# A hybrid attention block: last products of a stick-breaking pair moved behind the next pair's first units, and three kinds of DMA moved to another queue

## The chip, the cores and the metric

The kernel runs on one core of one Trainium2 chip. The metric is the time on the device in microseconds (us), the median of several runs. Before the change it is 1302.98 us (three runs, 1301.31 to 1303.53).

The core has five engines that run side by side and wait for each other by semaphores: PE (TensorE, matrix products and transposes, results in the banks of PSUM), DVE (VectorE), ACT (ScalarE), POOL (GpSimd) and SP (SyncE, which only issues DMAs here). Each engine goes through its own list of instructions in the order in which the program has them there. An instruction that waits holds what stands behind it in that list, and that goes for an instruction that issues a DMA too.

## The reference

One layer of a decoder: 1024 tokens, width 1024, all in float32.

```
h = rmsnorm(x);  proj = h @ w_in                      # 1024 x 3072
# group A, 8 heads of 64: q and k normed and rotated; three dilated branches
#   (window, dilation) = (128,1), (512,4), (2048,16), merged by their softmax denominators
# group B, 8 heads of 64, stick-breaking:
#   beta = sigmoid(q.k/8);  a[t,s] = beta[t,s] * prod_{s<j<t} (1 - beta[t,j]),  s < t;  o = a @ v
x = x + concat(rmsnorm(o_A), rmsnorm(o_B)) @ w_out
x = x + (silu(n @ w_gate) * (n @ w_up)) @ w_down      # n = rmsnorm(x), inner width 2816
```

## The kernel before

A float32 product is made of three products of rounded parts (`mm3`, lines 90 to 95: high by high, high by low, low by high), so each operand is first split by ACT (a copy that rounds) and DVE or POOL (the rest). The program runs in stages: norm and the projections of v, q and k of group A (to about 175 us of the profile), four pairs of heads of group A (175 to 362), four pairs of group B (348 to 588), the last output products and the second norm (to 659), the feed-forward part with Strassen-like combinations (649 to 1300).

The two attention groups use less of PE than the rest, so other products are mixed in as background: the projections of group B (`project_ahead`, tile pp) and the output products of group A (`merge_a`, tile yo). The main loop (lines 771 to 788) draws them from a generator: each `yield` of `attend_a` or `attend_b` reports how much of a pair is done, on a scale where a whole pair is about 24, and the loop lets background out in proportion (`RATES`), and the steps that prepare the next pair's q, k and v (`prep`, `FILL`). `hold` keeps a background product behind the score product that was written last before it.

The order of the instructions on an engine is not the order of the text. A planner (line 1186, `schedule_with_timeline_sim=True`) lays the whole program out along a modelled timeline when it is built; the text gives the priority, and what the model shows as ready goes first. So an instruction can stand ahead of one that the text has before it, and a transfer that takes longer than in the model holds what was placed behind it.

Group B, one pair of heads (`attend_b`, line 645). For each of 8 blocks of 128 queries and each head s a unit (`unit_b`, line 546) makes scores of n = 128 to 1024 keys (L430, L431, L433, tile sc), two sigmoids on ACT (L552, tiles kp and pb), a running product backwards over the keys on DVE (L555, the scan; its first operand is kp, the second is a column of zeros that is spread out, `aside`), and the product of the two, on POOL for s = 0 and on DVE for s = 1 (L556). kp has three buffers. Blocks go by twos, which are called groups g = 0 to 3; a group's four pb tiles are three of tag P (six buffers) and one of tag E (two). `ptpv` (line 559) then transposes the pb of a group (L572, tile pt), takes the transposes out of PSUM with ACT (L574, tile th) and multiplies them with v (L581, tile pv). In the text a group's `ptpv` comes after the next group's units, and the last group's at the end of the pair.

`aside` is one column in a PSUM bank of tag t. That tag has one bank, which group A uses as an accumulator; the bank is taken over at the start of the first pair of group B and filled by L649. In the last pair of group A the accumulator is taken out by L512.

Group A (`attend_a`, line 619). Per pair two halves of 512 queries, each in four steps. L449 and L450 make scores, DVE masks them and finds the maximum (L451), ACT takes the exponentials (L453), `turn_a` transposes (L498), takes out (L535, L537) and multiplies with v (L507). At the end of a half the sums and maxima are exchanged between layouts through DRAM (`factors`, line 455): st goes out (L460), comes back as x (L462), a few small operations make factors (`weigh`, L468 to L480), these go out (L481) and come back spread over partitions (`wide`, L486, two transfers). `finish` (line 611) multiplies on POOL (L615, L616) and stores the half (L617, tile oa). `weigh` and `finish` are due a fixed number of steps later (`WEIGH`, `USE`). All transfers of the kernel are issued by SP; the one at L462 waits for the two at L460, L486 for the one at L481, L617 for POOL. Behind them on SP stand, among others, the loads of rl, the stored projections for the next pair (L308, L311), which ACT and DVE turn into q and k (L339, L365, L340, L366), and the weights of the background (L69).

Of the kernel before, what the change touches and what calls it, by code (L numbers as in the profile page):

```python
# [11 lines left out]
F32 = mybir.dt.float32  # L12
FR = mybir.dt.float32r
AF = mybir.ActivationFunctionType
ALU = mybir.AluOpType
# [22 lines left out]
def tile_hybrid_block(ctx, tc, x, attn_norm_w, w_in, q_norm_w, k_norm_w, dil_w, sb_w,  # L38
                      w_out, ffn_norm_w, w_gate, w_up, w_down, cos, sin, amask, smask, out):
    nc = tc.nc  # L40

    big = ctx.enter_context(tc.tile_pool(name="big", bufs=1))

    def H(name, dtype=FR):
        return big.tile([128, 4, 512], dtype, tag="H", name=name, bufs=8)
# [4 lines left out]
    nc.vector.memset(ones, 1.0)  # L50
    mhalf = big.tile([128, 16], F32, name="mhalf")
    nc.vector.memset(mhalf, -0.5)
    def rstd_of(ss, n, pool, w):

        r = pool.tile([128, 16], F32, tag="rs", name="rs", bufs=6)
        nc.gpsimd.tensor_scalar(r[:, :w], ss, 1.0 / n, EPS, op0=ALU.mult, op1=ALU.add)
        nc.gpsimd.tensor_tensor(r[:, :w], r[:, :w], mhalf[:, :w], op=ALU.pow)
        return r
# [21 lines left out]
    def after(i, first, why, cls=mybir.DependencyClass.NoSync):  # L80

        tc.add_manual_dep(i.ins, first.ins.name,
                          mybir.DependencyInfo(cls, mybir.DependencyReason.DATA), reason=why)
# [47 lines left out]
    def P4(name, tag="P"):  # L131
        return att.tile([128, 1024], F32, tag=tag, name=name, bufs={"P": 6, "G": 2, "E": 2, "M": 1}[tag])
# [44 lines left out]
    def tok(w, tb, tag):  # L177

        p = PS.tile([128, 512], F32, tag, "va")
        c = slice((tb % 4) * 128, (tb % 4) * 128 + 128)  # L180
        for d in range(ND):
            h = hT[d // 4][tb // 4]
            mm3(p, (h[0][:, d % 4, c], h[1][:, d % 4, c]), (w[d // 2][0][:, d % 2, :], w[d // 2][1][:, d % 2, :]), d == 0, d == ND - 1)
        return p


    p = PS.tile([128, 512], F32, "s", "warm")
# [3 lines left out]
    for tb in range(NT):  # L191
# [14 lines left out]
        p = tok(wv, tb, "d")  # L206
        t = att.tile([128, 512], F32, tag="rq", name="rq", bufs=2)
# [20 lines left out]
    for nm, w in (("q", q_norm_w), ("k", k_norm_w)):  # L228
        t = P4("rope" + nm, "E").rearrange("p (s t e) -> p s t e", s=2, t=NT)
# [225 lines left out]
    def factors(st):  # L455


        sums = dram.tile([512, 2, 4], F32, name="sums")
        for l, order in enumerate(("(k p) l v -> p k l v", "(p k) l v -> p k l v")):
            nc.sync.dma_start(sums.rearrange(order, k=4)[:, :, l], st[:, l].rearrange("p k m s -> p k (m s)"))  # L460
        x = att.tile([128, 4, 2, 2, 2], F32, tag="x", name="x", bufs=2)
        nc.sync.dma_start(x.rearrange("p t l m s -> p t (l m s)"), sums.rearrange("(p t) l v -> p t (l v)", t=4))  # L462
        fac = dram.tile([2, 2, 512], F32, name="fac")

        def weigh():
            v = x.rearrange("p t l m s -> p l m s t")
            low = att.tile([128, 2, 4], F32, tag="low", name="low", bufs=2)
            i = nc.vector.tensor_tensor(low, v[:, 0, 0], v[:, 1, 0], op=ALU.min)  # L468
            after(i, gate[0], "the values are on their way")
            e = att.tile([128, 2, 2, 4], F32, tag="fe", name="fe", bufs=2)  # L470
            d = att.tile([128, 2, 2, 4], F32, tag="fd", name="fd", bufs=2)
            for l in range(2):
                nc.vector.tensor_tensor(e[:, l], low, v[:, l, 0], op=ALU.subtract)
            nc.scalar.activation(e, e, AF.Exp)
            for l in range(2):
                nc.vector.tensor_tensor(d[:, l], e[:, l], v[:, l, 1], op=ALU.mult)
            nc.vector.tensor_tensor(low, d[:, 0], d[:, 1], op=ALU.add)
            nc.vector.reciprocal(low, low)
            for l in range(2):
                nc.vector.tensor_tensor(e[:, l], e[:, l], low, op=ALU.mult)  # L480
            nc.sync.dma_start(fac.rearrange("l s (p t) -> p (l s) t", t=4), e.rearrange("p l s t -> p (l s) t"))  # L481

        def wide():
            t = P4("fac", "E").rearrange("p (l t) -> p l t", l=2)
            for s in range(2):
                nc.sync.dma_start(t[64 * s:64 * s + 64], fac[:, s].partition_broadcast(64))  # L486
            return t
        return weigh, wide

# [56 lines left out]
    def unit_b(pr, s, qb, tag):  # L546
        n = (qb + 1) * 128
        turn[0] += 1
        p, kp = P4("pb", tag), P4("kp", "GGM"[turn[0] % 3])
        for sp, c0, c1 in scores(pr, s, qb):  # L550
            for t, scale in ((kp, -0.125), (p, 0.125)):
                i = nc.scalar.activation(t[:, c0:c1], sp, AF.Sigmoid, scale=scale)  # L552
                after(i, last_exp[0], "one activation table at a time")
        rv = kp[:, n - 1::-1] if n == 1024 else kp[:, :n][:, ::-1]
        nc.vector.tensor_tensor_scan(rv, rv, aside[0][:, 0:1].to_broadcast([128, n]), 1.0, op0=ALU.mult, op1=ALU.bypass)  # L555
        (nc.gpsimd, nc.vector)[s].tensor_tensor(p[:, :n - 1], p[:, :n - 1], kp[:, 1:n], op=ALU.mult)  # L556
        return p

# [52 lines left out]
    def finish(pr, hf, o, wide):  # L611
        f = wide()
        t = pr.o[hf]
        for l in range(2):
            nc.gpsimd.tensor_tensor(t[l], t[l], f[:, l], op=ALU.mult)  # L615
        nc.gpsimd.tensor_tensor(t[0], t[0], t[1], op=ALU.add)  # L616
        nc.sync.dma_start(o[:, 512 * hf:512 * hf + 512], t[0])  # L617

    def attend_a(pr, o):

# [21 lines left out]

    aside = [None]

    def attend_b(pr, o):

        if aside[0] is None:
            aside[0] = PS.tile([128, 512], F32, "t", "aside")
            nc.vector.memset(aside[0][:, 0:1], 0.0)  # L649
        late = None  # L650
        for g in range(4):
            pq = []
            for k in range(2):
                pq.append([unit_b(pr, s, 2 * g + k, "PPPE"[2 * k + s]) for s in range(2)])
                catch_up(2)
                yield 0.2 * (2 * g + k + 1)
            if late:
                while pend:
                    catch_up(9)
                ptpv(*late)  # L660
                yield 0.92 * (2 * late[1] + 1.5)
            late = (pr, g, pq, o)
        ptpv(*late)
        yield 0.92 * (2 * late[1] + 1.5)

    def out_parts(g, i, hf, o, parts, acc):

# [139 lines left out]
    def wide(name, tag):  # L807
        t = att.tile([128, 1024], FR, tag=tag, name=name, bufs=BUFS[tag])
        return [t[:, 0:512], t[:, 512:1024]]
# [6 lines left out]
    for key, tags in (("b11", "PPPP"), ("b21", "PPvv")):  # L816
        t = [att.tile([128, 2, 512], FR, tag=tag, name=key, bufs=BUFS[tag]) for tag in tags]
# [78 lines left out]
    g = [None] * NF  # L896
# [143 lines left out]
    for ft in range(NF - LATE, NF):  # L1040
        gate_up(ft)
        if NF - 1 - ft < 12 - LATE:
            k = ft - (NF - 12 + LATE)
# [9 lines left out]
    sums = [H("tk", F32) for _ in range(4)]  # L1053
# [3 lines left out]
    for tag, n in (("k2", 2), ("k2", 2), ("kh", 4)):  # L1057
        t = att.tile([128, 1024], F32, tag=tag, name="lk", bufs=n)
# [131 lines left out]
```

## Time and profile before

| | |
|---|---|
| median of three runs | 1302.98 us |
| the profiled execution's own time | 1305.24 us |
| its span, first to last instruction | 1303.5 us |
| mean granted clock of PE | 0.991 |
| PE busy | 1265.4 us, 97% of the span |
| DVE, ACT, POOL busy | 840.0, 621.6, 384.2 us |
| DMA packets | 171.42 MB on SP's queue |

The profile tells one execution. A line of a group reads: program line, engine, operation, tiles (written <- read), shapes, count, busy time, mean of one in ns, then the idle time of the engine just before, and what ended most of it. In the order of time: start, length, engine, line, operation, tiles, and in brackets the idle time before it with what ended it. SPq is SP's queue of DMA issues. PEclk or "clock" is the share of PE's full rate that the chip granted. Since PE's instructions overlap, a busy PE can still be one at half rate.

### The profile page before, as it was taken

How to read it: one execution, taken by the hardware profiler on the slowest of the kernel's cores; microseconds unless marked ns; L12 is line 12 of the kernel's file. 1: busy time of each engine (PE TensorE's matmuls, PEld its weight loads, DVE VectorE, ACT ScalarE, POOL GpSimd, SP SyncE). 2: the span in 40 equal slices, each digit the busy share in tenths (PEclk: the TensorE clock that was granted, in tenths of full speed). 3: DMA queues.
4: the chain of work that ended last, by engine and by line, in shares of the span. 5: the costliest groups of instructions: out<-in, count | busy, mean ns of one | idle time of the engine just before them, and what ended most of it. 6: DMA issues, size and time to landing. Idle time of an engine off the chain costs nothing.

```text
span 1303.5 us, 18281 instructions
## 1 busy us (share of the span) xinstructions
PE 1265.4 (97%) x6260; PEld 1000.3 (77%) x6260; DVE 840.0 (64%) x1412; ACT 621.6 (48%) x1305; POOL 384.2 (29%) x330
## 2 busy tenths in 40 slices
PE   8999999999889988999999999999999999999998
PEld 6888887776666766767888888888888887788886
DVE  5333346566477768654798676665546878986775
ACT  5431267776687777753565222233333223444443
POOL 3488622422224234243312222321222321100000
PEclk9999999999989999999999999999999999999999
DMA  9633143544414253132246545323456448403532
GB/s 275 221 114 113 59 120 100 132 132 131 124 57 114 72 178 123 41 126 85 73 130 218 175 151 168 102 84 103 133 150 197 127 147 313 165 17 112 195 138 81
DMA packets 189326, 172.59 MB, mean 132 GB/s; under 512 B 33713, under 2 KB 134193, under 8 KB 189233
## 3 DMA queue, kind: packets, MB, share of 16 engines
q1 hardware_dynamic: 189232, 171.42, 41.8%
q8 instruction: 49, 0.80, 0.3%
q14 instruction: 45, 0.36, 0.1%
HBM read 133.96 MB, written 37.42 MB: 131 GB/s over the span
## 4 chain that ended last, share of the span: by engine, by line
PE 86%; ACT 4%; DVE 4%; DMA 3%; issue 2%; POOL 0%; SPq 0%; DVEq 0%; ACTq 0%; POOLq 0%
PE yd L1090 15%; PE gu L94 11%; PE gu L95 11%; PE gu L91 11%; PE va L95 3%; PE va L94 3%; PE va L91 3%; PE pp L91 3%; PE pp L94 3%; PE pp L95 3%; PE yo L91 2%; PE yo L94 2%; PE yo L95 2%; PE pv L507 2%; PE pv L581 2%
## 5 line engine op out<-in xcount | busy, mean ns | idle before, releaser
L864 ACT ACTIVATE wh<-wr 128x512 fp32r<-128x512 f32 x132 | 83.4, 632 | 210.0 <-PE gu L94 175.5
L94 PE MATMUL gu<-t,wh 128*128 128x512 f32 x352 | 139.0, 395 | 0.0
L91 PE MATMUL gu<-t,wh 128*128 128x512 f32 x352 | 138.8, 394 | 0.0
L95 PE MATMUL gu<-t,wl 128*128 128x512 f32 x352 | 138.8, 394 | 0.0
L1090 PE MATMUL yd<-dl,dh 128*128 128x512 f32 x308 | 121.7, 395 | 2.2 <-DVE dl L865 2.2
L1090 PE MATMUL yd<-dh,dl 128*128 128x512 f32 x308 | 121.2, 393 | 0.0
L94 PE MATMUL gu<-b,wh 128*128 128x512 f32 x264 | 104.5, 396 | 0.0
L91 PE MATMUL gu<-b,wh 128*128 128x512 f32 x264 | 104.3, 396 | 0.0
L95 PE MATMUL gu<-b,wl 128*128 128x512 f32 x264 | 104.2, 396 | 0.0
L555 DVE TENSOR_TENSOR_SCAN kp<-kp,aside 128x128 f32<-128x128 f32 (+7 forms) x64 | 85.4, 1347 | 27.3 <-ACT kp L552 26.9
L865 DVE TENSOR_TENSOR wl<-wr,wh 128x512 fp32r<-128x512 f32 x105 | 80.2, 763 | 8.1 <-ACT wh L864 8.1
L1090 PE MATMUL yd<-dh 128*128 128x512 f32 x308 | 84.6, 395 | 0.0
L91 PE MATMUL pp<-hh,wh 128*128 128x512 f32 x192 | 78.6, 410 | 0.0
L91 PEld LDWEIGHTS gu<-t,wh 128*128 128x128 f32 x352 | 66.2, 188 | 15.8
L94 PEld LDWEIGHTS gu<-t,wh 128*128 128x128 f32 x352 | 66.1, 188 | 15.7
L95 PEld LDWEIGHTS gu<-t,wl 128*128 128x128 f32 x352 | 66.1, 188 | 15.7
L91 PE MATMUL va<-wt,hh 128*128 128x512 f32 x192 | 76.5, 400 | 1.3 <-ACT wt L152 1.1
L864 ACT ACTIVATE dh<-wd 128x512 fp32r<-128x512 f32 x55 | 34.8, 632 | 90.2 <-PE yd L1090 83.6
L95 PE MATMUL va<-wt,hl 128*128 128x512 f32 x192 | 76.2, 398 | 0.7 <-DVE hl L62 0.7
L94 PE MATMUL va<-wt,hh 128*128 128x512 f32 x192 | 76.1, 399 | 0.2 <-DVE wt L153 0.2
L94 PE MATMUL pp<-hl,wh 128*128 128x512 f32 x192 | 76.3, 397 | 0.0
L95 PE MATMUL pp<-hh,wl 128*128 128x512 f32 x192 | 76.3, 397 | 0.0
(214 smaller groups left out, 3067.4 us busy)
## 6 DMA issues: line engine op xcount, KB each, us to landing
wd<-in_w_down_dram SPq DMA_DIRECT2D x88, 256.0 KB, 2.7
wr<-in_w_gate_dram SPq DMA_DIRECT2D x80, 256.0 KB, 3.0
wr<-in_w_up_dram SPq DMA_DIRECT2D x60, 256.0 KB, 3.0
raw<-in_w_in_dram SPq DMA_DIRECT2D x48, 256.0 KB, 4.3
raw<-in_w_out_dram SPq DMA_DIRECT2D x32, 256.0 KB, 2.9
raw<-rq SPq DMA_DIRECT2D x24, 256.0 KB, 2.6
g<-gu SPq DMA_DIRECT2D x20, 256.0 KB, 5.5
xt<-in_x_dram SPq DMA_DIRECT2D x8, 512.0 KB, 6.9
```

Source lines behind the costliest of these rows:

```text
L91: i = nc.tensor.matmul(ps, a[0], b[0], start=first, stop=False)
L94: nc.tensor.matmul(ps, a[0], b[1], start=False, stop=False)
L95: return nc.tensor.matmul(ps, a[1], b[0], start=False, stop=last)
L507: nc.tensor.matmul(pr.acc[lay][64 * s:64 * s + 64, cols], v[:, 64 * s:64 * s + 64], th[:, c:c + n], start=first, stop=last)
L555: nc.vector.tensor_tensor_scan(rv, rv, aside[0][:, 0:1].to_broadcast([128, n]), 1.0, op0=ALU.mult, op1=ALU.bypass)
L581: i = nc.tensor.matmul(pr.pv[64 * s:64 * s + 64, c - n:c], pr.v[:, j, 64 * s:64 * s + 64], th[:, n * s:n * s + n], start=j == 0, stop=j == ...
L864: nc.scalar.activation(h, r, AF.Copy)
L865: two(n).tensor_tensor(l, r, f(h), op=ALU.subtract)
L1090: mm = nc.tensor.matmul(pp[k], a[x][:, c], b[y], start=not more and j == 0 and x + y == 0, stop=j == HF - 1 and x == 1, skip_group_check=True)
```

## The change

Three things. The last group's `ptpv` of a stick-breaking pair is kept in `late` across pairs and written, for the first three pairs, after the next pair's group 0 of units; the last pair writes its own at the end. `part` scales what the pairs report as done, so that each still comes to 24: the first pair has one `ptpv` less, the last one more. `aside` is taken over at the start of group 2 of the first pair, and until then the scans read a column of zeros in SBUF, `zero`, instead. And three kinds of DMAs of group A, x (L462), fac (L486) and oa (L617), are issued by POOL instead of SP; L460 and L481 stay on SP.

```diff
+    zero = big.tile([128, 1], F32, name="zero")
+    nc.vector.memset(zero, 0.0)
...
-        nc.sync.dma_start(x.rearrange("p t l m s -> p t (l m s)"), sums.rearrange("(p t) l v -> p t (l v)", t=4))
+        nc.gpsimd.dma_start(x.rearrange("p t l m s -> p t (l m s)"), sums.rearrange("(p t) l v -> p t (l v)", t=4))
...
-                nc.sync.dma_start(t[64 * s:64 * s + 64], fac[:, s].partition_broadcast(64))
+                nc.gpsimd.dma_start(t[64 * s:64 * s + 64], fac[:, s].partition_broadcast(64))
...
-        nc.vector.tensor_tensor_scan(rv, rv, aside[0][:, 0:1].to_broadcast([128, n]), 1.0, op0=ALU.mult, op1=ALU.bypass)
+        nc.vector.tensor_tensor_scan(rv, rv, (aside[0] if aside[0] is not None else zero)[:, 0:1].to_broadcast([128, n]), 1.0, op0=ALU.mult, op1=ALU.bypass)
...
-        nc.sync.dma_start(o[:, 512 * hf:512 * hf + 512], t[0])
+        nc.gpsimd.dma_start(o[:, 512 * hf:512 * hf + 512], t[0])
...
+    late = [None]
+
     def attend_b(pr, o):
 
-        if aside[0] is None:
-            aside[0] = PS.tile([128, 512], F32, "t", "aside")
-            nc.vector.memset(aside[0][:, 0:1], 0.0)
-        late = None
+
+        part = 24.0 / (23.8 - 6.9 * (pr.i == 0) + 6.9 * (pr.i == 3))
         for g in range(4):
+            if aside[0] is None and g == 2 and pr.i == 0:
+                aside[0] = PS.tile([128, 512], F32, "t", "aside")
+                nc.vector.memset(aside[0][:, 0:1], 0.0)
             pq = []
             for k in range(2):
                 pq.append([unit_b(pr, s, 2 * g + k, "PPPE"[2 * k + s]) for s in range(2)])
                 catch_up(2)
-                yield 0.2 * (2 * g + k + 1)
-            if late:
+                yield part * 0.2 * (2 * g + k + 1)
+            if late[0]:
                 while pend:
                     catch_up(9)
-                ptpv(*late)
-                yield 0.92 * (2 * late[1] + 1.5)
-            late = (pr, g, pq, o)
-        ptpv(*late)
-        yield 0.92 * (2 * late[1] + 1.5)
+                ptpv(*late[0])
+                yield part * 0.92 * (2 * late[0][1] + 1.5)
+            late[0] = (pr, g, pq, o)
+        if pr.i == 3:
+            ptpv(*late[0])
+            yield part * 0.92 * (2 * late[0][1] + 1.5)
```

## The prediction

> **What bounds the kernel now.** I read the page first, for the engine that ends last, then the busy time by stage, then who ended PE's waits, and then the order of time around the longest of them. On the page the busy line and the shares of the chain are
>
> ```profile
> PE 1265.4 (97%) x6260; PEld 1000.3 (77%) x6260; DVE 840.0 (64%) x1412; ACT 621.6 (48%) x1305; POOL 384.2 (29%) x330
> PE 86%; ACT 4%; DVE 4%; DMA 3%; issue 2%; POOL 0%; SPq 0%; DVEq 0%; ACTq 0%; POOLq 0%
> ```
>
> PE is idle for 38.1 us of 1303.5. The change removes no product, so it can only win some of that, and whatever PE loses to a lower clock. The view by stretches shows where (length, busy us of each engine, PEclk near the end of the row). The dilated group is at work from 175 to 350, the stick-breaking pairs from 350 to 590; rows of it are
>
> ```profile
> core 0: us, PE busy (x) PEld busy (x) DVE busy (x) ACT busy (x) POOL busy (x), PEclk, DMA share, GB/s
> 175.00:300.00 125.00, 124.98 (x847) 96.42 (x845) 73.34 (x286) 95.80 (x281) 35.41 (x30) 1.00 0.45 117
> 300.00:350.00 50.00, 47.41 (x311) 35.49 (x310) 28.04 (x101) 33.42 (x100) 14.89 (x11) 0.97 0.40 118
> 350.00:367.00 17.00, 8.81 (x56) 6.24 (x55) 8.54 (x17) 9.96 (x22) 2.26 (x3) 0.71 0.48 126
> 460.00:510.00 50.00, 41.80 (x258) 29.80 (x257) 36.10 (x33) 41.19 (x91) 21.55 (x16) 0.97 0.49 172
> ```
>
> From 175 to 300 PE is busy all the time and nothing can be won; from 300 on it has holes. Its waits between 290 and 610 (us in total, times, longest) are
>
> ```profile
> PE pv L507 <- ACT th L535: 6.0, 2, 5.0
> PE pt L572 <- ACT th L574: 5.2, 3, 3.8
> PE sc L430 <- ACT pb L552: 4.6, 8, 1.3
> PE pt L572 <- DVE pb L556: 2.4, 3, 1.5
> PE pt L572 <- POOL pb L556: 2.3, 2, 1.7
> ```
>
> with 4.5 us in smaller rows: 25.0 of the 38.1 us. The rest lies at the start and in the last product, which the change doesn't touch. The stalls also cost clock. Four stretches with PEclk at one half:
>
> ```profile
> 312.80:316.20 3.40, 3.40 (x13) 2.57 (x10) 2.28 (x12) 3.06 (x12) 1.28 (x1) 0.50 0.23 78
> 357.20:370.80 13.60, 8.39 (x33) 6.52 (x34) 10.22 (x17) 10.36 (x23) 3.12 (x4) 0.50 0.21 66
> 466.40:469.80 3.40, 3.40 (x19) 2.68 (x16) 2.37 (x5) 3.40 (x10) 0.00 (x1) 0.50 0.89 331
> 565.40:568.80 3.40, 3.17 (x8) 2.50 (x9) 3.40 (x6) 2.12 (x4) 2.35 (x2) 0.50 0.73 222
> ```
>
> PE is busy for 18.36 us of them at half rate, so 9.2 us are lost. Stalls and clock together, 34 us, are the most that could be won.
>
> **The transition, 350 to 367.** In order of time (start, length, and in brackets the idle time before and what ended it):
>
> ```profile
> 349.86 0.33 SPq L617 DMA_DIRECT2D oa<-o  x1
> 350.25 0.43 SPq L460 DMA_DIRECT2D sums<-st  x1
> 351.37 1.09 SPq L311 DMA_DIRECT2D rl<-raw  x2
> 357.02 0.63 ACT L365 ACTIVATE kh<-rl 128x512 fp32r<-128x512 f32 x1 [4.36 <-DMA rl<-raw]
> 359.51 0.60 ACT L535 ACTIVATE th<-pt 128x512 f32<-128x512 f32 x1
> 360.16 1.97 PE L507 MATMUL pv<-th,v 128*64 128x256 f32 x12 [5.02 <-ACT th L535]
> 363.67 0.06 DVE L649 MEMSET aside<- 128x1 f32 x1 [0.43 <-ACT o L512]
> 364.87 0.48 PE L572 MATMUL pt<-ident,pb 128*128 128x128 f32 x1 [1.69 <-POOL pb L556]
> ```
>
> PE waits 5.0 us for an evacuation (L535) that stands on ACT behind a copy for a later pair (L365), and that one waits for its load, issued at 351.4. SP had stood at L617, which waits for POOL's sum, since 345.6, and then let seven transfers go in 4.4 us.
>
> **Part 1, the zero column.** One more fill of 128x1, 0.06 us as the one above, at the start, where DVE is idle: nothing. It frees the eight scans of the first pair's groups 0 and 1 from the fill of `aside`, which came at 363.67 because its bank belonged to the dilated group until then. The two waits for POOL's pb, 1.69 and 0.6, the row of 2.3 above, go: **-2.3** (bounds 0 and -2.3). What is late next is the second unit's sigmoid, which needed one of three kp buffers that these scans held; it is freed with them. The scans now read all their operands from SBUF, which no row shows; the nearest are the scans of before themselves, and I take them as equal; what eight small ones could lose beside POOL's products lies inside the bounds of part 2.
>
> **Part 2, the moved DMAs.** Per half of a pair one x, two fac and one oa: 32 issues leave SP. What SP stood waiting in front of them over the run, and the longest landing among them (KB, us):
>
> ```profile
> SPq L462 <- DMA sums<-st: 19.2, 8, 3.8
> SPq L617 <- POOL o L616: 17.9, 6, 4.2
> SPq L486 <- DMA fac<-fe: 15.5, 7, 3.0
> fac<-fac SPq DMA_DIRECT2D x16, 256.0 KB, 4.1
> ```
>
> That is 52.6 us in which loads of rl, weights and stores of rq stood behind them. The wait at L481 for fe stays on SP. Between 175 and 300 PE has no idle time to give back. At the transition the load at 351.37 can go earlier by 0 (its buffer is free only then, or the burst of sums<-st holds its landing) to 4.3 us (all of SP's stand from 345.6 to 349.9); I take 1.5, about a third, as the chain behind it keeps its other load waits: **-1.5** of the 5.0 (bounds 0 and -5.0). With 5.0 down to 3.5 and part 1's holes gone I let the half-rate stretch lose one piece of 3.4 us: **-1.7** (bounds 0 and -4.2, half of its 8.39 busy us). In the last dilated pair SP shows the same pattern, L617 at 301.33 and then a load that ACT waits for:
>
> ```profile
> 308.41 1.29 ACT L339 ACTIVATE qs<-rl 64x512 fp32r<-64x512 f32 x2 [2.00 <-DMA rl<-raw]
> 312.45 0.83 PE L507 MATMUL pv<-th,v 128*64 128x256 f32 x4 [1.01 <-ACT th L535]
> ```
>
> PE's stalls there are 2.6 us (300:350 above); half of them, **-1.3** (bounds 0 and -4.3, with the half-rate piece at 312.8).
>
> On POOL an issue is not to be seen. Its price lies between SP's 0.33 us and a POOL product's 1.31 us (the row below), so 11 to 42 us for 32; POOL is busy for 65 of the 228 us from 175 to 403, and idles 69.8 us in front of L615 for the very data that these transfers bring:
>
> ```profile
> L615 POOL TENSOR_TENSOR o<-o,fac 128x512 f32<-128x512 f32 x16 | 20.7, 1311 | 69.8 <-DMA fac<-fac 61.2 <-ACT pa L453 8.6
> ```
>
> Behind a waiting issue stand POOL's splits of weights (L74), the regrouped queries (L346) and, in the first stick-breaking pair, L556. The tile that `finish` hands back is wanted two halves later. For the first half of all,
>
> ```profile
> 217.31 0.33 SPq L617 DMA_DIRECT2D oa<-o  x1
> 239.61 0.60 ACT L512 ACTIVATE o<-pv 128x512 f32<-128x512 f32 x1
> ```
>
> 22 us lie between the issue and the evacuation that writes that buffer again, so even 4 issues of 1.31 and a slower landing are covered; were that cover gone, PE would wait for what exceeds it. I charge one issue, the mean of the two prices, in front of one L556: **+0.8** (bounds 0 and +3, a wait for sums as in L462's mean of 2.4 with its issue).
>
> **Part 3, the late products.** The transposes and products with v of a pair's group 3 now stand behind the next pair's units 0 and 1 in program text, and `part` spreads background and preparation over what each pair then has. The planner reorders already; the rows are the three boundaries, and two sigmoids of units 0 and 1:
>
> ```profile
> 407.61 0.22 PE L430 MATMUL sc<-kh,qs 128*128 128x128 f32 x1
> 410.69 0.65 PE L572 MATMUL pt<-ident,pb 128*128 128x128 f32 x4 [1.14 <-ACT th L574]
> 463.24 1.28 ACT L339 ACTIVATE qs<-rl 64x512 fp32r<-64x512 f32 x2 [3.95 <-DMA rl<-raw]
> 465.20 0.66 PE L572 MATMUL pt<-ident,pb 128*128 128x128 f32 x4 [3.76 <-ACT th L574]
> 505.01 0.51 PE L430 MATMUL sc<-kh,qs 128*128 128x512 f32 x1 [1.28 <-ACT pb L552]
> 465.04 0.27 ACT L552 ACTIVATE kp<-sc 128x128 f32<-128x128 f32 x1
> 360.48 0.39 ACT L552 ACTIVATE kp<-sc 128x256 f32<-128x256 f32 x1
> ```
>
> At 465 an evacuation again stands behind a copy that waits for its load. The stalls at the three boundaries are 1.5 us (1.14 and the next at 411.67), 3.8 with a half-rate piece that lost 1.7, and 3.7 (1.28 and five smaller ones from 495 to 511): 10.7. With units 0 and 1 ahead, their scores are available to fill such a hole, and preparation moves to an earlier place in the pair, because the late products now count 6.9 of 24 right after unit 1. But the loads keep their waits, so I take a fifth: **-2.0** (bounds -10.7 and +9.6, worked out in the last rival).
>
> **Sum.** -2.3 - 1.5 - 1.7 - 1.3 + 0.8 - 2.0 = -8.0 us. Against the profiled execution's 1305.24 us (span 1303.5) that is 1297.2; that execution lies 2.3 us over the median of 1302.98, so the median should come to **1295.0**.
>
> By the page "TensorE: Matmul & The Clock Gate" of the Trainium skill, section "Part 1: The HAM clock gate", the rate halves after an idle window of about 3.4 us. By that rule a stall of 3.5 us would seldom hold a whole window, the stretch from 357.2 would go, and the sum would be an estimated -10.5, 1292.5 us. The trace speaks against it: the half-rate piece at 312.8 follows two stalls of 0.85 and 1.01 us.
>
> **The rivals.** (a) Releasing SP brings nothing: ACT waits for landings, not issues. For it: the load issued at 351.37 was awaited until 357.02, with sums<-st in flight beside it; against it: 52.6 us of standing. Then -2.3 + 0.8 - 2.0 = -3.5, 1299.5 us. The Trainium skill's "DMA: Bandwidth & Descriptors", section "Issuing engines are not separate DMA queues", says that issuing from several engines saves only the time of issue, which gives the same. (b) Part 3 does not do what it says, since the planner had already put scores of the next pair ahead of these products (407.61 against 410.69): its term is 0, 1297.0 us. (c) The loads of prepared pairs keep every stall and only part 1 counts: -2.3 + 0.8 = -1.5, 1301.5 us. (d) Slower: the late products are now late. With units 0 and 1 their group holds all six P and both E buffers, and unit 2 can't start before they give theirs back; twelve score products and eight sigmoids now stand in front of them, four of 0.27 and four of 0.39 us, 2.6 us on ACT at each of three boundaries: +7.9, and one more half-rate piece, +1.7. With parts 1 and 2 that is -6.0 + 7.9 + 1.7 = +3.6, 1306.6 us. It decides where ACT has no idle time to take the sigmoids in, while PE waits for the last unit's product. For it: ACT is busy 41.2 of 50 us from 460 to 510; against it: at 407.6 a score of the next pair stands in front already, and before 463.24 ACT was idle for 3.95 us.
>
> **How the numbers follow.** The forecast has 0.37, with a range of its own from 1289 to 1299. The rivals have (a) 0.17, (b) 0.13, (c) 0.15, (d) 0.18. No change is within 0.2%, 2.6 us, about what a measurement of this kernel can tell. Faster: 0.37 + 0.13 + most of (a), 0.13, so 0.63; within: (c) and the rest of (a), 0.19; slower: (d), 0.18. The range leaves out a tenth on each side: from 1287, about half of all boundary and transition bounds won beyond the sum, to 1307, just over (d).
>
> **What would show it.** Right: the scans of the first pair run from about 352 instead of 363.8, no wait for `aside`; SP's waits at L462, L486 and L617 are gone and POOL's are there; the stall at the transition is 3 to 4 us and the half-rate stretch shorter; the boundary stalls sum to under 9 us. Wrong: PE waits for POOL's pb longer than 2.3 us, half-rate stretches of more than the 23.8 us shown, or holes in 175 to 300, where there are none.

## The result, and the profile after

The changed kernel takes 1296.7 us (median of 20 runs, 1294.9 to 1301.1), the kernel before 1303.7 us on the same chip. The ratio is 0.9945, with a 95% interval of 0.9937 to 0.9954: 7.0 us faster. The forecast was 1295.0 us. The profiled execution took 1295.6 us, its span is 1293.8. In code that both kernels have, line numbers are 2 to 6 higher than before.

The busy line of the page, the same stretches as in the prediction, and PE's waits from 290 to 610 us (us in total, times, longest), all of the changed kernel:

```profile
PE 1261.8 (98%) x6260; PEld 997.2 (77%) x6260; DVE 838.9 (65%) x1413; ACT 620.3 (48%) x1305; POOL 404.8 (31%) x362
```

```profile
175.00:300.00 125.00, 122.93 (x825) 94.70 (x825) 70.31 (x279) 92.62 (x274) 43.91 (x46) 0.99 0.44 114
300.00:350.00 50.00, 48.31 (x326) 36.31 (x325) 29.59 (x107) 35.29 (x104) 20.82 (x20) 1.00 0.49 125
350.00:367.00 17.00, 12.89 (x83) 9.23 (x83) 14.55 (x21) 14.24 (x34) 6.93 (x7) 1.00 0.50 140
460.00:510.00 50.00, 45.31 (x278) 32.64 (x277) 36.37 (x36) 41.22 (x92) 22.91 (x18) 0.97 0.35 123
```

```profile
PE sc L432 <- ACT pb L554: 8.2, 12, 1.4
PE pt L574 <- DVE pb L558: 1.2, 3, 0.5
PE pt L574 <- ACT th L576: 1.1, 2, 0.6
PE pv L509 <- ACT th L537: 1.0, 2, 0.6
```

The transition from 350 to 367 has 12.89 us of products instead of 8.81, at full clock instead of 0.71. PE's waits for ACT's evacuation of the dilated group (6.0 us, one of them 5.0) are down to 1.0, and the longest wait shown is 1.4. Its waits for pb in front of the next scores (L432) went up, from 4.6 to 8.2, in short pieces. One stretch got worse: from 175 to 300, where PE had no hole, it now idles 2.07 us. The order of time around both places, first the hole that is new, then the transition:

```profile
237.04 2.53 POOL L617 TENSOR_TENSOR o<-o,fac 128x512 f32<-128x512 f32 x2 [6.74 <-DMA fac<-fac]
239.53 1.30 POOL L76 TENSOR_TENSOR wl<-raw,wh 128x512 fp32r<-128x512 f32 x1
240.77 0.61 POOL L464 DMA_DIRECT2D x<-sums  x1
245.45 0.17 DVE L470 TENSOR_TENSOR low<-x 128x8 f32<-128x8 f32 x1 [4.39 <-DMA x<-sums]
245.54 0.42 DVE L539 COPY th<-pt 128x256 f32<-128x256 f32 x1
246.01 0.44 PE L509 MATMUL pv<-th,v 128*64 128x128 f32 x4 [1.58 <-DVE th L539]
246.90 0.66 PE L509 MATMUL pv<-th,vc 128*64 128x128 f32 x8 [0.45 <-ACT th L537]
...
350.52 1.09 SPq L313 DMA_DIRECT2D rl<-raw  x2
352.74 0.39 PE L432 MATMUL sc<-kh,qs 128*128 128x256 f32 x1 [0.73 <-ACT pb L554]
352.94 0.74 DVE L557 TENSOR_TENSOR_SCAN kp<-kp,zero 128x128 f32<-128x128 f32 x2
354.32 0.65 PE L509 MATMUL pv<-th,v 128*64 128x256 f32 x4 [0.67 <-DVE th L539]
354.72 0.63 ACT L367 ACTIVATE kh<-rl 128x512 fp32r<-128x512 f32 x1 [1.20 <-DMA rl<-raw]
357.99 0.45 PE L432 MATMUL sc<-kh,qs 128*128 128x384 f32 x1 [1.26 <-ACT pb L554]
359.26 0.65 PE L509 MATMUL pv<-th,v 128*64 128x256 f32 x4 [0.60 <-ACT th L537]
```

At 246 PE waits for a tile copy of DVE (L539). That stands behind L470, which waits for x, and x could be issued only at 240.77: on POOL it stood behind the product that waits for fac until 237.04, and behind a split of weights. In the kernel before, SP issued this x at 238.40, and there was no hole. At the transition the one stall of 5.0 us has become four of 0.6 to 1.3 us, and two under 0.5 behind them. The scans run from 352.94, not 363.76, and ACT waits for its load 1.20 us, not 4.36 (and 1.41 for the next).

What the three DMAs cost POOL as issues (us in total, mean ns of one), and where POOL now stands for them (us, times, longest):

```profile
L488 POOL DMA_DIRECT2D fac<-fac x16 | 9.7, 610 | 44.4 <-DMA fac<-fe 41.7 <-PE pt L574 2.7
L464 POOL DMA_DIRECT2D x<-sums x8 | 4.9, 612 | 16.8 <-DMA sums<-st 12.4 <-DVE kp L557 3.2 <-PE sc L452 1.1
L619 POOL DMA_DIRECT2D oa<-o x8 | 4.7, 587 | 1.6 <-POOL o L618 1.6
```

An issue takes POOL 0.6 us, 19.3 us for all 32. POOL stands 54.1 us at fac and x.

To compare kernels by place I cut the time in which the change acts into three: the dilated group (160 to 335 us), the transition (335 to 378) and the pairs (378 to 645). In each, a kernel loses the time in which PE is idle, and half of PE's busy time while its clock is at one half. The rows of the changed kernel and of the kernel before, whose first two numbers give the idle time (175.00 - 171.24 = 3.8 us) and whose PEclk gives the clock:

```profile
160.00:335.00 175.00, 171.24 (x1114) 131.78 (x1113) 96.66 (x357) 124.48 (x359) 65.80 (x67) 0.99 0.46 121
335.00:378.00 43.00, 38.24 (x259) 28.57 (x259) 31.93 (x66) 34.13 (x86) 15.20 (x15) 1.00 0.41 110
378.00:645.00 267.00, 256.09 (x1436) 194.75 (x1436) 187.17 (x205) 178.91 (x382) 94.53 (x83) 0.99 0.30 101
```

```profile
160.00:335.00 175.00, 172.40 (x1120) 132.58 (x1118) 98.13 (x364) 126.14 (x362) 51.09 (x42) 0.99 0.45 122
335.00:378.00 43.00, 34.60 (x219) 26.47 (x219) 23.68 (x53) 28.68 (x73) 10.48 (x10) 0.84 0.34 98
378.00:645.00 267.00, 252.38 (x1423) 190.79 (x1420) 188.92 (x204) 179.76 (x384) 93.23 (x77) 0.99 0.31 102
```

With the half-rate pieces of 3.4 us that lie in each stretch (before: 1, 4, 2; after: 1, 0, 2), the losses are 4.3, 12.6 and 17.9 us before, and 5.5, 4.8 and 14.3 after. That is 10.3 us less in sum. The two profiled executions differ by 9.6 us, the medians by 7.0: a place tells of one execution.

### The profile page after: what moved, and what is told of

The parts are those of the page before. It is cut to its first block, busy times and chain, and to the rows that moved or that the text cites. A ratio compares the mean times of both kernels' runs of the same rounds, so it can differ in the third digit from the quotient of the medians.

```text
span 1293.8 us, 18298 instructions
## 1 busy us (share of the span) xinstructions
PE 1261.8 (98%) x6260; PEld 997.2 (77%) x6260; DVE 838.9 (65%) x1413; ACT 620.3 (48%) x1305; POOL 404.8 (31%) x362
## 4 chain that ended last, share of the span: by engine, by line
PE 58%; DVE 3%; DMA 2%; issue 1%; ACT 1%; POOL 0%; DVEq 0%; SPq 0%; ACTq 0%; POOLq 0%
PE yd L1096 15%; PE gu L96 11%; PE gu L97 11%; PE gu L93 11%; PE yo L93 2%; PE yo L96 2%; PE yo L97 2%; PE pv L583 1%; PE pt L574 1%; DMA g<-gu 1%; DMA wd<-in_w_down_dram 1%; DVE kp L557 1%; PE sc L432 1%; PE ptr L112 1%; PE sc L433 0%
## 5 line engine op out<-in xcount | busy, mean ns | idle before, releaser
L557 DVE TENSOR_TENSOR_SCAN kp<-kp,aside 128x640 f32<-128x640 f32 (+7 forms) x56 | 78.8, 1421 | 29.6 <-ACT kp L554 29.4
L871 POOL TENSOR_TENSOR wl<-wr,wh 128x512 fp32r<-128x512 f32 x27 | 39.0, 1446 | 124.4 <-ACT wh L870 114.0
L870 ACT ACTIVATE dh<-wd 128x512 fp32r<-128x512 f32 x55 | 34.8, 632 | 89.8 <-PE yd L1096 81.8
L93 PE MATMUL va<-wt,hh 128*128 128x512 f32 x192 | 76.5, 400 | 1.1 <-ACT wt L154 0.9
```

The source lines that it names most:

```text
L93: i = nc.tensor.matmul(ps, a[0], b[0], start=first, stop=False)
L557: nc.vector.tensor_tensor_scan(rv, rv, (aside[0] if aside[0] is not None else zero)[:, 0:1].to_broadcast([128, n]), 1.0, op0=ALU.mult, op1 ...
L870: nc.scalar.activation(h, r, AF.Copy)
L871: two(n).tensor_tensor(l, r, f(h), op=ALU.subtract)
```

## The experiments

**Each part alone.** Theory S was that SP's standing at the three waits held ACT at the transition, and that the late products do little; rival L, that the late products carry the gain; rival N, that any edit makes the planner lay the work out anew, and the gain is the luck of that.

The DMAs alone, in the kernel before:

```diff
-        nc.sync.dma_start(x.rearrange(...
+        nc.gpsimd.dma_start(x.rearrange(...
-                nc.sync.dma_start(t[64 * s:64 * s + 64], fac...
+                nc.gpsimd.dma_start(t[64 * s:64 * s + 64], fac...
-        nc.sync.dma_start(o[:, 512 * hf:512 * hf + 512], t[0])
+        nc.gpsimd.dma_start(o[:, 512 * hf:512 * hf + 512], t[0])
```

> The kernel before with the three DMAs on POOL alone. Theory S (what held ACT at the transition was SP standing at these waits, and the late products add little): 3 to 5 us faster than before, PE's stall of 5.0 us at 355 to 360 down to under 3.5, and the new hole of some 2 us near 246 that the changed kernel has, since x stands on POOL behind POOL's own waits. Rival L (the late products carry the gain): within 1.3 us of before. Rival N (each edit re-plans everything, and what comes out is a draw): anywhere within 4 us, and the parts alone don't add up to the 7.0 us of the whole.

Measured: 1308.2 us, ratio 1.0019 (1.0004 to 1.0034), slower by 2.5 us. The late products alone (`late` across pairs, `part`):

```diff
-            late = (pr, g, pq, o)
-        ptpv(*late)
+            late[0] = (pr, g, pq, o)
+        if pr.i == 3:
+            ptpv(*late[0])
...
```

> The kernel before with the late products and part alone; aside is taken over at the start as before, all DMAs on SP. Theory S: 1 to 3 us faster, the stall of 5.0 us at the transition is still there, the boundary stalls shrink from 9.0 us to 5 or 6. Rival L: 5 to 7 us faster. Rival N: no tie to the boundaries.

Measured: 1301.9 us, ratio 0.9977 (0.9965 to 0.9989). The zero column alone (`aside` taken over at group 2 of the first pair):

```diff
-... aside[0][:, 0:1].to_broadcast([128, n]) ...
+... (aside[0] if aside[0] is not None else zero)[:, 0:1].to_broadcast([128, n]) ...
...
```

> The kernel before with the zero column alone, aside taken over at group 2. Theory S: 1.5 to 3 us faster; PE's two waits for POOL's pb, 2.3 us, go, the 5.0 us stall stays. Rival L: within 1.3 us of before, as the stall of 5.0 us covers what is won. Rival N: anywhere within 4 us.

Measured: 1303.5 us, ratio 0.9982 (0.9967 to 0.9998). And one of the planner's rates moved, in the kernel before, with nothing else:

```diff
-LEAD, PRE, RATES = 18.0, 17.0, (15.0, 18.0, 18.0, 18.0, 15.0, 17.0, 15.0, 18.0)
+LEAD, PRE, RATES = 18.0, 17.0, (15.0, 18.0, 18.0, 18.0, 15.5, 17.0, 15.0, 18.0)
```

> The kernel before with one pacing number changed, the background of the first stick-breaking pair 15.5 in place of 15.0: nothing that any part of the change touches. Theory S and rival L: within 1.3 us of before. Rival N: 3 us or more to either side, with holes in other places than before.

Measured: 1306.7 us, ratio 1.0003 (0.9987 to 1.0019). This one new layout brings nothing, which speaks against rival N. Rival L, with 5 to 7 us for the late products, fell: alone they bring 3.0 by their ratio. Theory S fell too: the DMAs alone make the kernel slower. They do shorten the stall at the transition (5.0 to 3.3 us), but with the rate alone moved it was 3.9. The three sum to -2.8 us, and together they measure -7.0. So pairs of parts were to be run.

**Two parts each, and x back on SP.** x back, in the changed kernel:

```diff
-        nc.gpsimd.dma_start(x.rearrange(...
+        nc.sync.dma_start(x.rearrange(...
```

> The changed kernel with the load of x back on SP; fac and oa stay on POOL. Theory Q (POOL's queue works in order, and the changed kernel's hole at 246 us comes from x, which stands on POOL behind the product that waits for fac until 237.0 and is issued at 240.8): the hole of 1.58 + 0.45 us and the half-rate piece at 248 go, and nothing takes their place: 2.0 + 1.7 = 3.7 us less than the changed kernel, about 1293.0, ratio to before 0.9917. Rival W (SP's standing is what held the transition): SP again stands at x, 19.2 us over the run, and the stall at 352 to 364 comes back in part (2 us or more in one piece, the load of rl landing later than 354.7): as much as the changed kernel or up to 3 us more, 1296.7 to 1299.7. Rival N (the order of execution falls anew with every edit): the hole moves elsewhere, 1296.7 within 1.5.

Measured: 1295.0 us, ratio 0.9922 (0.9899 to 0.9945), near theory Q's 0.9917; rival W's stall did not come back (none over 1.2 us from 343 to 366). The interval reaches to the changed kernel's 0.9945, so this was run again below. Zero column and late products, with all three kinds of DMAs back on SP:

```diff
-        nc.gpsimd.dma_start(x.rearrange(...
+        nc.sync.dma_start(x.rearrange(...
-                nc.gpsimd.dma_start(t[64 * s:64 * s + 64], fac...
+                nc.sync.dma_start(t[64 * s:64 * s + 64], fac...
-        nc.gpsimd.dma_start(o[:, 512 * hf:512 * hf + 512], t[0])
+        nc.sync.dma_start(o[:, 512 * hf:512 * hf + 512], t[0])
```

> Parts 1 and 3, all DMAs on SP. The parts alone measured -2.3 (zero column), -3.0 (late products) and +2.5 us (DMAs), -2.8 in sum, against -7.0 for all. Theory I (the DMAs pay only where the other two parts are in: alone they uncover the wait for pb that the zero column removes): without them the kernel loses 1.5 to 3 us of the gain, 1298.2 to 1299.7, ratio 0.9960 to 0.9970, with a stall of 2 us or more in one piece at 352 to 364 and no hole at 246. Rival M (the DMAs cost 2.5 us here too, and the zero column and the late products together gain more than their sum): 1294.2, ratio 0.993. Rival A (all additive): 1298.4, ratio 0.9960, which only the next two runs tell from theory I.

Measured: 1298.9 us, ratio 0.9953 (0.9934 to 0.9971). Late products and DMAs, the scans reading `aside` from the start:

```diff
-... (aside[0] if aside[0] is not None else zero)[:, 0:1] ...
+... aside[0][:, 0:1] ...
...
```

> Parts 2 and 3; the scans of the first pair wait for the fill of aside again. Additive: +2.5 - 3.0 = -0.5, 1303.2 us, ratio 0.9996. Theory I: the transition's stall is short but the waits for POOL's pb (2.3 us) and the half-rate stretch from 357 stay, since the late scans come at 362 or later: as much as late products alone or a little more, 1301 to 1303. Rival M (late products and DMAs together make the gain): 1299 or less, ratio 0.9965 or less.

Measured: 1301.1 us, ratio 0.9961 (0.9948 to 0.9974). Zero column and DMAs, each pair writing its own last products:

```diff
-            late[0] = (pr, g, pq, o)
-        if pr.i == 3:
-            ptpv(*late[0])
+            late = (pr, g, pq, o)
+        ptpv(*late)
...
```

> Parts 1 and 2; the late products stay in their own pair. Additive: -2.3 + 2.5 = +0.2, 1303.9 us, ratio 1.0002. Theory I: the transition comes out as in the changed kernel (no stall over 1.5 us from 350 to 367, no half-rate stretch there), so about 5 us are won against the DMAs alone, while the stall of 3.7 us at the second boundary (466) with its half-rate piece stays and the holes of the dilated group stay: 1300 to 1301.5, ratio 0.9975 to 0.9985. If the transition's stretch stays at half rate, the late products matter there too, and theory I falls.

Measured: 1303.0 us, ratio 0.9980 (0.9965 to 0.9996). All eight combinations, with the losses by place, in us, worked out as above for each profiled execution, and the time against the kernel before (the ratio by 1304 us):

| parts | dilated | transition | pairs | sum | time, 95% interval |
|---|---|---|---|---|---|
| none (before) | 4.3 | 12.6 | 17.9 | 34.8 | 0 |
| none, one rate moved | 4.2 | 10.2 | 18.4 | 32.7 | +0.4 (-1.7 to 2.5) |
| DMAs | 8.0 | 10.2 | 17.4 | 35.5 | +2.5 (0.5 to 4.4) |
| late | 4.4 | 11.9 | 13.2 | 29.5 | -3.0 (-4.6 to -1.4) |
| zero | 4.2 | 7.9 | 17.0 | 29.2 | -2.3 (-4.3 to -0.3) |
| zero, DMAs | 6.0 | 5.5 | 19.1 | 30.6 | -2.6 (-4.6 to -0.5) |
| late, DMAs | 5.5 | 11.0 | 13.4 | 29.9 | -5.1 (-6.8 to -3.4) |
| zero, late | 2.6 | 8.0 | 13.8 | 24.4 | -6.1 (-8.6 to -3.8) |
| all (after) | 5.5 | 4.8 | 14.3 | 24.5 | -7.2 (-8.2 to -6.0) |
| all, run again (below) | 5.7 | 5.6 | 14.5 | 25.7 | -8.0 (-9.9 to -6.0) |
| all, x on SP | 1.7 | 5.3 | 16.4 | 23.4 | -10.2 (-13.2 to -7.2) |
| all, x on SP, run again (below) | 1.8 | 5.5 | 14.5 | 21.8 | -9.8 (-11.6 to -8.1) |

A place moves by itself, too: the rate alone moved the transition's loss by 2.4 us, and second profiles of one kernel differ by up to 1.9 in a place. Against that, each part has its own. The late products win 3.2 to 4.8 us in the pairs, in all four comparisons. The zero column wins 3.9 to 6.2 at the transition, in all four. The DMAs lose 1.1 to 3.7 in the dilated group; at the transition they win 0.9 to 3.2, with the same sign in all four but hardly more than the rate moved there. In the sum that is about nothing. The times say the same within their intervals: zero and late add up (-5.3 apart, -6.1 together), and the DMAs change the other three rows by -2.1 to -0.3 us, which these runs can't tell from nothing. Whether they cost 2.5 us alone or the 0.7 that the places show stays open; that profile also has two half-rate pieces elsewhere (at 17 and 1095 us), as other executions have.

Theory I gave the right ratio for zero with DMAs and the wrong one for late with DMAs (1301 to 1303 us there, a ratio of 0.998 or more; 0.9961 was measured). That run met rival M's number (0.9965 or less), but by place it loses as much as the late products alone (29.9 and 29.5 us), and for zero and late without DMAs M had 0.993, where 0.9953 was measured. Theory I's reason isn't shown by place: at the transition the DMAs win 2.4 us without the zero column and 2.4 with it where the late products are out, 0.9 and 3.2 where they are in, and that difference is no larger than what the rate alone moved. No run shows that a part needs another; the excess of -7.0 over -2.8 is mainly the +2.5 of the DMAs alone, which no other comparison shows again.

What the DMAs win at the transition, from the order of time of zero and late without them:

```profile
355.16 0.63 ACT L367 ACTIVATE kh<-rl 128x512 fp32r<-128x512 f32 x1 [4.41 <-DMA rl<-raw]
...
356.99 0.69 PE L432 MATMUL sc<-kh,qs 128*128 128x384 f32 x1 [3.39 <-ACT pb L554]
```

ACT stands 4.41 us for the load, and PE 3.39; with the DMAs on POOL these were 1.20 and 1.26. From 335 to 378 PE is idle for nearly as long in both (5.1 us here, 4.8 there); what differs is that most of it lies in one piece here, and two half-rate pieces follow.

By the clock the load is issued no earlier with the DMAs on POOL (its second half at 349.78 here, at 351.03 in the changed kernel). But the changed kernel comes to this place late, by its hole at 246 us and the half-rate piece behind it: the same half of the load before this one is issued at 343.19 here and at 346.05 there. From that load to this one it is 6.6 us here and 5.0 there. With x back on SP (`e4_x_on_sp`), and so without the hole, the two loads are

```profile
341.60 1.09 SPq L313 DMA_DIRECT2D rl<-raw  x2
345.78 1.09 SPq L313 DMA_DIRECT2D rl<-raw  x2
```

and the second half of the second, at 346.28, comes 3.5 us earlier than the 349.78 here (2.8 in the second profile of that kernel). The load also lands sooner after its issue: in 5.3 us here, in 3.7 in the changed kernel. SP stood here at the store to oa until 347.76 and then let seven transfers go within 4 us, which would be a reason, but it isn't shown. Over all profiles this landing took 4.7 to 5.3 us in the five without a moved DMA, 2.9 to 4.0 in the eight with both fac and the store on POOL, and 5.2 in the one with the store alone there (below), where SP did not stand at it.

**The price on POOL.** The changed kernel again, and three variants of it, on one chip. First the changed kernel itself:

> The changed kernel itself, on the same chip as the next three, so that they can be set against it. Every theory: ratio to before 0.9945 within 0.0015, some 1296.5 us.

Measured: 1297.8 us, ratio 0.9939 (0.9924 to 0.9954). With x on SP, as above:

> The changed kernel with the load of x on SP, against the changed kernel on the same chip. Theory Q (x behind the waiting product on POOL makes the hole at 246 us): 2 to 3.7 us below the changed kernel, ratio to before 0.992 to 0.993. Rival N (the gain of the first look was scatter between chips): within 1 us of the changed kernel.

Measured: 1295.7 us, ratio 0.9925 (0.9911 to 0.9938). x is issued 3.0 us earlier, and DVE no longer waits for it:

```profile
237.79 0.33 SPq L464 DMA_DIRECT2D x<-sums  x1
...
241.37 0.99 DVE L470 TENSOR_TENSOR low<-x 128x8 f32<-128x8 f32 x1
```

```profile
160.00:335.00 175.00, 173.19 (x1136) 133.34 (x1134) 102.11 (x372) 127.42 (x367) 61.92 (x60) 1.00 0.48 124
335.00:378.00 43.00, 39.16 (x252) 29.19 (x251) 30.70 (x53) 34.04 (x84) 16.58 (x14) 0.96 0.41 114
```

The hole at 246 and its half-rate piece are gone, and the dilated group is down to 1.8 us of idle time and no half rate: 3.9 us of loss less than the changed kernel beside it (5.7), at a transition that stays as it was (5.5 against 5.6). The hole of 1.5 us or more near 246 is in all six profiles that have x on POOL (both of the changed kernel, the three runs with the DMAs and without one or both other parts, and the last variant below) and in none of the eight without. Of the 3.9 us the medians show 2.1, and theory Q is borne out in its place and sign.

Only the store to oa on POOL, x and fac on SP:

```diff
-        nc.gpsimd.dma_start(x.rearrange(...
+        nc.sync.dma_start(x.rearrange(...
-                nc.gpsimd.dma_start(t[64 * s:64 * s + 64], fac...
+                nc.sync.dma_start(t[64 * s:64 * s + 64], fac...
```

> Parts 1 and 3, and of the three DMAs only the store to oa on POOL; x and fac stay on SP. Theory Q: a store that stands on POOL right behind the sum that it stores waits for nothing and blocks nothing, so there is no hole at 246 and the load of rl at the transition comes as early as in the changed kernel (SP no longer stands at L619, 18.1 us without part 2): as fast as with x alone on SP, ratio 0.992 to 0.993. Rival F (the wait for fac, 15.0 us of SP's standing, matters as much): the stall at the transition stays at 2 us or more in one piece, ratio 0.994 to 0.9955, as with no DMA moved.

Measured: 1295.5 us, ratio 0.9927 (0.9912 to 0.9943). As fast as with fac moved too, so fac makes no difference that shows in the time, and x loses. Rival F's stall of 2 us in one piece isn't there (1.67 at most). By place this profile loses 4.1, 7.1 and 14.8 us, with two half-rate pieces at the transition; its execution is the slowest of the six (1300.0), so whether fac has a part in these stays open. With no DMA moved the ratio was 0.9953, on another chip and with an interval that touches this one, so what the store alone wins stays open. Both variants are 2 us under the changed kernel beside them by their medians, with intervals that overlap its own, and they are the fastest that were run.

The last variant puts the zero column in front of every scan, for a reason that the changed kernel's own profile gives. Two scans of 384 there, in one row, with POOL beside them:

```profile
362.30 1.50 POOL L683 TENSOR_TENSOR acc<-acc,sq 128x512 f32<-128x512 f32 x1 [3.41 <-ACT sq L682]
...
362.68 2.81 DVE L557 TENSOR_TENSOR_SCAN kp<-kp,zero 128x384 f32<-128x384 f32 x2
```

The first of the two took 1.93 us, the second 0.95, as scans of this size take with `aside`.

```diff
-... (aside[0] if aside[0] is not None else zero)[:, 0:1].to_broadcast([128, n]) ...
+... zero[:, 0:1].to_broadcast([128, n]) ...
```

> The changed kernel, with every scan of the stick-breaking pairs reading the zero column in SBUF (the fill of the bank stays, for nothing). In the changed kernel the 384-wide scan at 362.7, which reads it, took 1930 ns while POOL added into acc (L683), its neighbour beside a pb product of POOL 947 ns; scans that read aside in PSUM beside the same addition took their usual time. Theory P (a scan with all operands in SBUF is held up by POOL's addition into acc): the scans that meet this addition later, three in the changed kernel, at 472, 483 and 489, take 1 us or more longer, the others nothing; DVE is off the path for most of it, so the time rises by 0 to 3 us. Rival (the one long scan was held up by something else, such as the fill of aside issued behind it): no scan is longer, the time is the changed kernel's within 1 us.

Measured: 1310.0 us, ratio 1.0031 (1.0019 to 1.0043): 12.2 us slower than the changed kernel on the same chip, four times the most that was expected. Most of it is lost in the pairs: 25.2 us against 14.5, and 36.9 against 25.7 over the three places. The rival expected no scan to be longer, and fell. The widest scans, in the changed kernel of that chip and in this one, and two rows of this one's order of time:

```profile
L557 DVE TENSOR_TENSOR_SCAN kp<-kp,aside 128x1024 f32<-128x1024 f32 x8 | 18.2, 2278 | 0.6 <-ACT kp L554 0.5
```

```profile
L557 DVE TENSOR_TENSOR_SCAN kp<-kp,zero 128x1024 f32<-128x1024 f32 x8 | 27.4, 3429 | 0.1
```

```profile
450.35 2.41 POOL L558 TENSOR_TENSOR pb<-pb,kp 128x1023 f32<-128x1023 f32 x1 [6.65 <-DVE kp L557]
...
450.93 3.98 DVE L557 TENSOR_TENSOR_SCAN kp<-kp,zero 128x1024 f32<-128x1024 f32 x1
```

It is not only the addition into acc: a scan that begins while POOL works on a product has to wait for it. POOL ends at 452.76, 1.83 us after the scan's start; with a usual 2.28 that makes 4.11, and 3.98 were taken. At 362.68 it is 1.12 + 0.95 = 2.07 against 1.93. The Trainium skill says this in "SBUF — State Buffer", section "SBUF: two separate sides": a VectorE operation with two inputs in SBUF and a GpSimd operation share one pair of ports, and who starts first holds it for its whole instruction. For scans that start second the trace agrees, within 0.15 us in both cases, and in all 18 scans of the last variant that begin beside a running product of POOL. Scans that read `aside` in PSUM don't show it: in the kernel before, those of 1024 took 2.27 to 2.29 us, all eight.

## Why the prediction was right, and where not

**The sum and the range.** -8.0 was forecast, -7.0 measured, and the time lies in the forecast's own range. The signs that were named for it came: scans from about 352 (352.94), waits for POOL's pb of 0.6 instead of 2.3, the boundaries' stalls shorter. The transition's longest stall came out at 1.3, where 3 to 4 was named. One sign that was named for wrong came too: holes in 175 to 300. That the sum is so near is in part luck. Parts 1 and 3 were to win 4.3 us and won 6.1 together (3.8 to 8.6); part 2 was to win 3.7, all its terms taken together, and brought 1.1 on top of them, which the intervals don't tell from nothing. Two errors of opposite sign nearly cancel.

**Part 1, -2.3.** Alone -2.3 in time. But its place shows more than the two waits that the step counted: at the transition the losses fall by 4.7 us, since the long stall falls from 5.0 to 2.4 us and two of the four half-rate pieces go. The prediction gave that to part 2. That scans of SBUF alone cost the same held for seven of the eight; one took 1 us more, and in the 18 us behind it PE waits no longer than 0.65 us at once. The bound that was put to this price, inside part 2's, holds for eight small scans only: with the other 56 as well the kernel takes 12 us more.

**Part 2 at the transition, -1.5 and -1.7.** The stall was to shrink by 1.5 and one half-rate piece to go. The DMAs move the losses there by -0.9 to -3.2 us, so the forecast is the upper end of what they do; the rest of the transition's gain (7 to 8 us with part 1's) is part 1's. The reason holds: where no hole stands against it the load is issued 2.8 to 3.5 us earlier, inside the bounds of 0 to 4.3, and it lands sooner after its issue, which the prediction did not have. In 300 to 350 the idle time fell from 2.59 to 1.69, 0.9 of the 1.3 forecast. But this goes with x, not with the store that the step named: it is 1.6 to 1.8 us in the six profiles with x on POOL, which have the hole at 246, and 2.4 to 3.4 in the eight without.

**Part 2 on POOL, +0.8: the step that failed.** The price of an issue, 0.6 us, lies between the two bounds. But the lower one, 0.33, was read from a store to oa; the issues of fac, half of the 32, took 0.60 us on SP as well. The step named what stands behind a waiting issue on POOL, and found 22 us of cover for the finished tile. It did not ask what the issue itself stands behind. x waits on POOL for a product that waits for fac; DVE waits for x with a tile copy behind it, and PE for that copy. "From 175 to 300 nothing can be won" was read as nothing to lose. There the change loses 2.0 us of idle time and a half-rate piece, 3.7 us in all, and the variant with x on SP has them back.

**Part 3, -2.0.** Alone -3.0 (-4.6 to -1.4), 3.2 to 4.8 us by place. The stall of 3.76 at the second boundary is gone. The fifth of 10.7 us was too careful, and its reason, that the loads keep their waits, is wrong. ACT's waits for rl from 378 to 600 us, before and with the late products alone:

```profile
ACT kh L365 <- DMA rl<-raw: 8.0, 3, 3.7
ACT qs L339 <- DMA rl<-raw: 6.5, 3, 4.0
```

```profile
ACT qs L341 <- DMA rl<-raw: 2.5, 1, 2.5
ACT kh L367 <- DMA rl<-raw: 2.2, 1, 2.2
```

14.5 us became 4.7. They are 14.1 to 15.0 in all five profiles without part 3 and 2.4 to 4.9 in all nine with it. The step had named what may be the cause, that preparation moves to an earlier place in the pair, but gave it no weight; no run took that apart from the rest of part 3.

**The rivals.** (b), the planner had done it, and (d), late products late, fell with the run of part 3 alone. (c), only part 1 counts, fell with the same run. (a), releasing SP brings nothing, is false by place and nearly true in the sum: with zero and late in, the three DMAs brought 1.1 us that the intervals don't separate from none. That ACT waited for a landing was its true half, but how long a landing takes changed with the DMAs as well. What the Trainium skill says of this ("DMA: Bandwidth & Descriptors", section "Issuing engines are not separate DMA queues"), that other issuing engines save only issue time, is less than the trace shows: here they also let the load that stood behind them go earlier, and add waits of their own.

## What to carry to other kernels

Before a waiting DMA moves to another engine's queue, look at what stands ahead of it there as well as behind it: a store right behind its own sum waits for next to nothing (1.6 us in all eight), a load behind a product that waits for something else comes late. A stretch in which the bounding engine has no hole can't win, but it can lose, so its place in the sum is a bound on one side, not a zero. And when three edits go in together, cut the time by place and compare there, with a second profile of one kernel to say how far a place moves by itself: the medians of the parts alone added up to -2.8 and would have told a story that the places don't bear out.

## What was not expected of the hardware

**The clock goes by a grid.** In each of the fourteen profiles all half-rate pieces between 160 and 645 us begin on a grid of 3.413 us. Five such windows of the changed kernel, in pairs or alone (length, PE busy, and PEclk, third number from the end):

```profile
244.60:248.00 3.40, 1.54 (x16) 1.13 (x17) 2.04 (x14) 1.68 (x6) 0.73 (x1) 1.00 0.23 86
248.00:251.40 3.40, 3.40 (x12) 2.61 (x12) 0.78 (x4) 2.06 (x8) 0.41 (x1) 0.50 0.31 80
357.30:360.70 3.40, 2.12 (x16) 1.36 (x18) 2.76 (x4) 3.33 (x8) 1.28 (x2) 1.00 0.23 72
452.80:456.20 3.40, 1.66 (x13) 1.18 (x11) 3.27 (x5) 3.38 (x10) 0.00 (x0) 1.00 1.03 417
456.20:459.60 3.40, 3.40 (x11) 2.73 (x10) 3.26 (x7) 1.77 (x6) 0.41 (x1) 0.51 0.72 250
```

A window with 1.86 or 1.74 us of idle time is followed by one at half rate; that at 357.3, with 1.28, is not. Over all fourteen profiles, of the windows at full clock 32 had more than 1.72 us idle, and all 32 were followed by half rate; of 79 with 1.0 to 1.72 us, 18; of some 1800 with less, none. So more than half a window of idle time, summed over its stalls, always cost the clock, less than 1 us never, and what decides between the two stays open. By these counts one stall would cost the clock or not by where it falls on the grid. The prediction quoted the Trainium skill's rule that a whole idle window of about 3.4 us is needed ("TensorE: Matmul & The Clock Gate", section "Part 1: The HAM clock gate"). The length agrees; the idle time that was enough is half of it, and in 18 cases less. It fits the transition, where the 5.0 us are now spread, and four half-rate pieces became none in one profile of the changed kernel and one in the other.

**POOL as an issuer.** An issue of x or oa held POOL for 612 and 587 ns, against 337 and 355 on SP; one of fac held both alike, 610 and 604. The transfers landed later after their issue: x 3.0 us in the median (2.1 from SP), fac 4.4 (4.1), oa 3.4 (2.1).
